# Token factors without a DRAM round trip, four raw and four split weight buffers, values in column halves, head norms on GpSimd's DMA queue: a two-layer hybrid encoder on one Trainium2 core

## The chip, the cores and the metric

One program on one core of one Trainium2 chip. The metric is the device time of one execution in microseconds (us), lower is better. Five engines work at once, each on its own queue in order: PE (TensorE, matmul), DVE (VectorE), ACT (ScalarE), POOL (GpSimd) and SP (SyncE, which here issues DMAs).

## What is computed

Input x is (1, 512, 1024) in float32, so 512 tokens with 1024 columns. Two layers, then a final RMSNorm:

```
h = rmsnorm(x, norm_w)
aq, ak, av, ag, bq, bk, bv, bg, cu, cg = split(h @ w_in)          # 4608 columns
A: 4 heads, two softmax maps each: p = softmax(q k^T / 8 + bias); o = (p0 - lam * p1) @ av; rmsnorm per head; * silu(ag)
B: 4 heads of retention, forward and backward scan with decay, summed; rmsnorm per head; * silu(bg)
C: 4 groups, centred means over 2/4/8/16 tokens minus the token, a 128x128 map, a scale; * silu(cg)
x = x + concat(A, B, C) @ w_out                                    # 1536 rows
```

## The kernel before

**Precision by splitting.** Products run in the array's 4-byte float32r format. Every operand is split into a rounded high part and the rest, `split` (line 453): ACT casts to the high part, DVE subtracts to get the low one. A product is then three matmuls (`mm3`, line 499). So each weight costs one DMA into a raw buffer, one ACT cast and one DVE subtraction before PE can use it.

**Weights.** They stream in granules of 512 KB, 128 partitions by 1024 columns, in the order in which the units use them (`granules`, line 424). `emit_granule` (line 428) loads one into one of 2 `wraw` buffers and splits it into one of WBUFS = 5 pairs `wh`, `wl` (line 25). `take` (line 443) hands out the next granules and records loads up to five granules ahead.

**Order of the work.** The body is recorded first, unit by unit, by the strings in ORDERS (line 32) with the priorities HIGH (line 40). Then a list scheduler (`schedule`, line 201) plays it through with the weights of `cost` (line 304) and the latencies of `LATENCY`, and fixes each engine's instruction order and each tile's buffer. Tiles of one tag get buffers first come, first served in recorded order. So a changed cost, buffer count or operand changes the order of everything after it. All instructions are emitted at line 1051, which is why the profile shows L1051 for nearly all rows; the tile names tell them apart.

**First unit.** `first_values` (line 702) starts layer 0 on x transposed times the norm weight, before the tokens' rms factors are known. START (line 27) is its own order: k0 to k7 are the eight 128-row blocks of x^T with their matmuls, x0 to x3 load the four token tiles and compute their factor into `rc` (128 partitions, one column per tile), R spreads the 512 factors along the free axis into `rb` (128 x 512, every partition the same), V stores the values. R (lines 734 to 737) writes `rc` to DRAM, one 4-byte element at a time in token order, and reads that row back to all partitions, both on SP's queue. `scaled_T` (line 752), `rotated` (line 773) and `c_pool` (line 895) multiply by `rb` in layer 0.

**Values.** `values` (line 694) makes av, and bv of layer 1: 128 tokens are the stationary operand, 512 weight columns move, all four granules of the unit are held at once, and `proj_tok` (line 509) and `store_values` (line 743) go through the four token tiles. The other projections (`proj_T`, line 515) keep 128 weight columns stationary and move 512 tokens.

**Head norm.** `headnorm` (line 538) ends each of the 8 A and 8 B heads: copy out of PSUM, four transposes, squares summed by ACT, a power of -1/2 on POOL, and then the 512 factors go to DRAM and come back to all partitions in `rb`, again on SP's queue, for one DVE multiplication `og<-og,hn`:

```python
        nc.gpsimd.tensor_tensor(st[:, 4:8], st[:, 0:4], neghalf, op=ALU.pow)
        row = nc.tile("dram", "row", [S], 4, F32)
        nc.sync.dma_start(row.rearrange("(p j) -> p j", j=4), st[:, 4:8])
        rb = o
        nc.sync.dma_start(rb, row.partition_broadcast(P))
```

**Attention.** In `a_head` (line 865) one DVE instruction adds the bias to the logits and takes the row maximum, a second one negates that maximum, and ACT takes the exponential with it as its bias.

Of the kernel before, what the change touches and what calls it, by code (L numbers as in the profile page):

```python
# [15 lines left out]
P = 128  # L16
# [8 lines left out]
WBUFS = 5  # L25
# [4 lines left out]
# Order in which the units of a layer are recorded. An output unit is named by the pairs of 128-row blocks of w_out that it takes  # L30
# (A: P Q, B: R S, C: T U) and its half of the columns.
# [7 lines left out]
# how far the units of a kind are moved ahead  # L39
# [4 lines left out]
# The kernel body is recorded first, on tiles that have no place yet. A list scheduler then fixes the order in which  # L44
# every engine issues its instructions and the slot each tile takes, and the program is emitted in that order.
# [17 lines left out]
class View:  # L63
    """Part of a recorded tile: partitions p0..p1, free offsets idx, and the steps that lead to it."""
# [32 lines left out]
    def window(self, row, first, pattern):  # L97
        """DRAM only: elements of a row from first on, by an access pattern of its own."""
        return View(self.base, self.p0, self.p1, self.idx, self.steps + (("window", row, first, pattern),))

    def spread(self, n):
        """Every element n times, along a new last axis."""
        return View(self.base, self.p0, self.p1, np.repeat(self.idx[..., None], n, -1), self.steps + (("spread", n),))
# [47 lines left out]
class Recorder:  # L151
# [49 lines left out]
    def schedule(self):  # L201
# [39 lines left out]
        def ready(op):  # L241
            """A PSUM bank serves one engine at a time."""
            t = op.ready
            for b in op.banks:
                for e, end in b.last.items():
                    if e != op.engine:
                        t = max(t, end + latency(e, op.engine))
            return t
# [3 lines left out]
        while len(order) < len(self.ops):  # L252
# [14 lines left out]
            if e == "SP":  # L267
                bus = max(bus, start + 1100) + op.time
                op.end = bus + 908
# [28 lines left out]
WARM = 16  # matmuls on zeros at the start  # L298
QUEUE = 8  # transfers under way in a queue
FINE = 2  # weight granules of the first columns that come in two parts  # L300
# [3 lines left out]
def cost(engine, method, args, kw):  # L304
    """What an instruction weighs for the list scheduler: until its result stands, and on its engine."""
    out = args[0]
    n = out.idx.size if isinstance(out, View) else 0
    psum = any(isinstance(a, View) and a.base.space == "psum" for a in args)
    if engine == "PE":
# [5 lines left out]
        t = max(107, n * 0.417) + 2.5  # L315
        return t, t
    if engine == "SP":
# [3 lines left out]
        return nbytes / 360.0, 475  # L321
    if engine == "DVE":
# [10 lines left out]
        elif method == "memset":  # L333
            t = 9
        else:
            t = 1.041 * max(n, 2) + 75
        return t, t
    if engine == "ACT":
# [3 lines left out]
        t += 93 * ("accum_out" in kw)  # L342
        return t, t
    if method == "tensor_tensor" and kw["op"] == ALU.pow:
        return 300 + 164 * n, 300 + 164 * n
# [5 lines left out]
def record(ins: dict, out: bass.AP):  # L351
# [46 lines left out]
    ident = sb("ident", [P, P])  # L398

# [6 lines left out]

    def g_out(l, e0, half):
        return w_out[l, e0:e0 + 256, HALF[half]].rearrange("(k p) c -> p k c", p=P)

    def unit_granules(l, u):  # L410
        if u in ("bv", "av"):
            return g_tok(l, BV if u == "bv" else AV)
# [15 lines left out]
    def emit_granule(parts=1):  # L428
        src = granules[len(wt)]
        shp = [P, src.shape[1], src.shape[2]]  # L430
        raw = sb("wraw", shp, 2)
# [11 lines left out]
    def take(n):  # L443
        i = wstate[0]
        wstate[0] += n
        while len(wt) < min(i + WBUFS, len(granules)):
# [12 lines left out]
    def square(t, half, junk, part=None):  # L459
        """Mean square of token tile t: the share of one half of its columns, or of a quarter in the second half."""  # L460
# [14 lines left out]
    def scaled(t, wb, dst, half):  # L475
        """One half of the columns of the rmsnorm of token tile t."""
# [3 lines left out]
    def transpose4(src, step=None):  # L480
        """Four 128-column blocks of src, each transposed, in one bank."""
# [22 lines left out]
    def mm_stacked(ps, qk, m, cols):  # L504
        """Full product of slot m's query columns with its keys: both query parts lie stacked on partitions."""
# [3 lines left out]
    def proj_tok(ps, gs, hh, hl, t):  # L509
        for k in range(KD):  # L510
            wh, wl = gs[k // 2]
            mm3(ps, hh[:, k, t * P:(t + 1) * P], hl[:, k, t * P:(t + 1) * P],
                wh[:, k % 2, :], wl[:, k % 2, :], k == 0, k == KD - 1)
# [8 lines left out]
    def stack_halves(dst, slots, src, scale, dup):  # L522
        """Split the 64 rows of each half of src. Without dup the low part goes to the other partition half of
        the same slot; with dup both parts take a slot each, present on both partition halves."""
# [13 lines left out]
    def headnorm(ov, scale, g):  # L538
        """ov * scale * rsqrt(mean over partitions of ov^2 + eps) * g"""
# [11 lines left out]
        nc.sync.dma_start(row.rearrange("(p j) -> p j", j=4), st[:, 4:8])  # L551
        rb = o
        nc.sync.dma_start(rb, row.partition_broadcast(P))
# [3 lines left out]
    def out_half(ms, half, after=None, before_end=None):  # L557
        """before_end: the last token tile comes in two quarters of the columns, and this follows the first."""
# [25 lines left out]
    def decay_tables():  # L584
        # retention decay rows: log_gamma on 8 partitions (layer, head), columns (forward, backward)
# [33 lines left out]
        # decay of a key to the border of its chunk that faces the other chunk, by token: columns (tile, layer, head)  # L619
# [7 lines left out]
    def column_tables():  # L627
        # per-channel columns: subln (2 rows), pool_scale (8 rows), with the gate's factor 1/2
# [7 lines left out]
    def bias_tables():  # L636
        # relative-position bias by distance
# [8 lines left out]
        for i in range(2):  # L646
            ps = lgp()
            nc.tensor.matmul(ps[0:4, :], rbs, ohr[0:64, HALF[i]], start=True, stop=True)
            nc.vector.tensor_copy(gsb[0:4, HALF[i]], ps[0:4, :])
        nc.sync.dma_start(gdram, gsb[0:4, :])  # L650

        # lambda of each layer
# [13 lines left out]
    def toeplitz(src, row):  # L666
        """t[p, 895 - j] = value at distance j - 384 - p"""
# [4 lines left out]
    def chunk_decay(row):  # L672
        """t[p, j, 255 - c] = decay at distance c - 128 j - p"""
# [4 lines left out]
    def toep_tile(t, i):  # L678
        """[p, c] = value at distance c - 128 i - p"""
        return t[:, i * P:i * P + S][:, ::-1]  # L680

# [1 line left out]
    class Layer:  # L683
# [10 lines left out]
        def values(self):  # L694
            self.vh, self.vl = sb("vh", [P, NT, 512], 1, F32R), sb("vl", [P, NT, 512], 1, F32R)
            gs = take(4)
            for t in range(NT):
                ps = pj()
                proj_tok(ps, gs, self.hh, self.hl, t)
                self.store_values(t, ps)  # L700

        def first_values(self):
            """Layer 0 runs on x^T w; its products take the token's rms afterwards."""
            self.vh, self.vl = sb("vh", [P, NT, 512], 1, F32R), sb("vl", [P, NT, 512], 1, F32R)
            self.rb, self.rc = sb("rb", [P, S]), edge[:, 28:32]
            # the clock of the PE array rises once it has been kept busy for a while
# [6 lines left out]
            for u in START.split():  # L713
# [20 lines left out]
                elif u[0] == "R":  # L734
                    row = nc.tile("dram", "row", [S], 4, F32)
                    nc.sync.dma_start(row.rearrange("(t p) -> p t", t=NT), self.rc)
                    nc.sync.dma_start(self.rb, row.partition_broadcast(P))
# [5 lines left out]
        def store_values(self, t, ps):  # L743
            hi, lo = self.vh[:, t, :], self.vl[:, t, :]
# [7 lines left out]
        def scaled_T(self, ps, scale=1.0):  # L752
            """A product in its final size."""
# [11 lines left out]
        def gate(self, key):  # L765
            """2 silu of the next 128 gate columns."""
# [6 lines left out]
        def rotated(self):  # L773
            """Next 128 columns (two heads), rotated."""
# [18 lines left out]
        def b_qk(self, pr):  # L793
            """Queries and keys of two heads; the state that each of the two chunks hands to the other one."""
# [64 lines left out]
        def a_qk(self, h):  # L859
            t = sb("qk", [P, 6, S], 2, F32R)  # L860
            stack_halves(t, 0, *self.scaled_T(proj_T(self.hh, self.hl), 0.125), False)
# [3 lines left out]
        def a_head(self, h):  # L865
# [3 lines left out]
            for half in range(2):  # L869
                ah, al = ttile([P, NT, 256], F32R), ttile([P, NT, 256], F32R)  # L870
                for i2 in range(2):
# [3 lines left out]
                    for mp in range(2):  # L875
# [3 lines left out]
                        nc.vector.tensor_tensor_reduce(s, lg, toep_tile(bt, i), scale=1.0, scalar=-3e38,  # L879
                                                       op0=ALU.add, op1=ALU.max, accum_out=st[:, mp:mp + 1])  # L880
# [233 lines left out]
```

## Time and profile before

| | before |
|---|---|
| timed runs, us | 682.1, 682.11, 685.32 (median 682.11) |
| span of the profiled execution, us | 679.9 |
| PE busy | 659.5 us, 97% |
| PE weight loads busy (beside PE) | 541.1 us, 80% |
| DVE busy | 500.7 us, 74% |
| ACT busy | 353.9 us, 52% |
| POOL busy | 30.3 us, 4% |
| mean granted PE clock | 0.994 of full speed |
| DMA | 71.86 MB, 106 GB/s over the span |

The span runs from the first to the last instruction. No separate time is given for the profiled execution; the median of the timed runs is 2.2 us above its span, and that is what lies around it. An engine's busy time counts an instruction from its start to its end; matmuls overlap their neighbours in the pipeline, so the rate of PE is read from starts of successive matmuls, not from the duration of one.

### The profile page before, as it was taken

How to read it: one execution, taken by the hardware profiler on the slowest of the kernel's cores; microseconds unless marked ns; L12 is line 12 of the kernel's file. 1: busy time of each engine (PE TensorE's matmuls, PEld its weight loads, DVE VectorE, ACT ScalarE, POOL GpSimd, SP SyncE). 2: the span in 40 equal slices, each digit the busy share in tenths (PEclk: the TensorE clock that was granted, in tenths of full speed). 3: DMA queues.
4: the chain of work that ended last, by engine and by line, in shares of the span. 5: the costliest groups of instructions: out<-in, count | busy, mean ns of one | idle time of the engine just before them, and what ended most of it. 6: DMA issues, size and time to landing. Idle time of an engine off the chain costs nothing.

```text
span 679.9 us, 8912 instructions
## 1 busy us (share of the span) xinstructions
PE 659.5 (97%) x3171; PEld 541.1 (80%) x3171; DVE 500.7 (74%) x954; ACT 353.9 (52%) x701; POOL 30.3 (4%) x51
## 2 busy tenths in 40 slices
PE   9969999999999999999999999899999999999996
PEld 7757887878788888887888888688888887888785
DVE  5468987787787998976574779767568957887733
ACT  7525673434376866553443756344447765655321
POOL 0000000000000000001010000000000000000011
PEclk9979999999999999999999999999999999999999
DMA  9447444323326223243322423532342143224302
GB/s 325 147 127 186 139 115 117 110 94 78 90 50 181 77 91 105 69 115 91 115 63 78 139 64 88 131 118 71 95 122 65 50 150 97 71 92 90 99 31 94
DMA packets 85141, 71.86 MB, mean 106 GB/s; under 512 B 6004, under 2 KB 67604, under 8 KB 85096
## 3 DMA queue, kind: packets, MB, share of 16 engines
q1 hardware_dynamic: 85096, 71.29, 36.3%
q8 instruction: 25, 0.41, 0.2%
q14 instruction: 20, 0.16, 0.1%
HBM read 69.09 MB, written 2.18 MB: 105 GB/s over the span
## 4 chain that ended last, share of the span: by engine, by line
PE 78%; DMA 10%; DVE 6%; issue 2%; ACT 2%; SPq 1%; POOL 0%; POOLq 0%; DVEq 0%; ACTq 0%
PE pj L1051 64%; PE lg L1051 6%; PE ov L1051 4%; PE tp L1051 4%; DMA hn<-row 3%; DMA wide<-dd 2%; DVE qk L1051 1%; DMA row<-edge 1%; DVE soft L1051 1%; DMA wraw<-in_w_in 1%; DVE wl L1051 1%; DMA cols<-in_scales 1%; DMA T<-in_xT_w 1%; DMA x<-in_x 1%; ACT soft L1051 1%
## 5 line engine op out<-in xcount | busy, mean ns | idle before, releaser
L1051 PE MATMUL pj<-hh,wh 128*128 128x512 f32 x448 | 178.5, 400 | 7.9 <-ACT wh L1051 6.5
L1051 PE MATMUL pj<-hl,wh 128*128 128x512 f32 x448 | 177.5, 397 | 0.0
L1051 PE MATMUL pj<-hh,wl 128*128 128x512 f32 x448 | 176.9, 396 | 0.0
L1051 ACT CAST wh<-wraw 128x1024 fp32r<-128x1024 f32 (+1 forms) x97 | 100.8, 1039 | 106.9 <-PE pj L1051 75.8
L1051 DVE TENSOR_TENSOR wl<-wraw,wh 128x1024 fp32r<-128x1024 f32 (+1 forms) x97 | 117.3, 1210 | 29.7 <-ACT wh L1051 29.1
L1051 PEld LDWEIGHTS pj<-hh,wh 128*128 128x128 f32 x448 | 84.7, 189 | 27.1 <-ACT wh L1051 7.0
L1051 PEld LDWEIGHTS pj<-hh,wl 128*128 128x128 f32 x448 | 84.6, 189 | 18.6
L1051 PEld LDWEIGHTS pj<-hl,wh 128*128 128x128 f32 x448 | 84.7, 189 | 17.7
L1051 PE MATMUL pj<-wh,mAC 128*128 128x512 f32 (+1 forms) x264 | 87.5, 391 | 0.0
L1051 ACT ACTIVATE soft<-soft,sm 128x512 f32<-128x512 f32 x96 | 67.8, 718 | 33.9 <-DVE sm L1051 33.5
L1051 DVE TENSOR_TENSOR x<-x,pj 128x512 f32<-128x512 f32 (+1 forms) x65 | 43.6, 675 | 23.2 <-PE pj L1051 22.8
L1051 PEld LDWEIGHTS pj<-wh,mAC 128*128 128x128 f32 x264 | 49.0, 188 | 10.3
L1051 PE MATMUL lg<-qk 128*128 128x512 f32 (+1 forms) x192 | 51.4, 361 | 1.5 <-DVE soft L1051 1.5
L1051 PE MATMUL pj<-wl,mAC 128*128 128x512 f32 (+1 forms) x132 | 51.4, 389 | 0.0
L1051 POOL TENSOR_TENSOR st<-st,neghalf 128x4 f32<-128x4 f32 (+1 forms) x28 | 25.1, 896 | 477.3 <-DVE st L1051 379.2
L1051 DVE CUSTOM_DVE_ANT_0 soft<-lg,wide 128x512 f32<-128x512 f32 x64 | 43.3, 687 | 1.9 <-PE lg L1051 0.3
L1051 PE MATMUL pj<-wh,mB 128*128 128x512 f32 (+1 forms) x136 | 44.5, 383 | 0.0
L1051 PE MATMUL pj<-wh,hl 128*128 128x512 f32 x104 | 41.4, 398 | 0.0
L1051 PE MATMUL pj<-wh,hh 128*128 128x512 f32 x104 | 41.3, 398 | 0.0
L1051 PE MATMUL pj<-wl,hh 128*128 128x512 f32 x104 | 41.2, 396 | 0.0
L1051 PEld LDWEIGHTS lg<-qk 128*128 128x128 f32 x192 | 32.5, 188 | 9.6 <-DVE soft L1051 2.5
L1051 PE MATMUL ov<-T,vh 128*128 128x256 f32 x192 | 39.1, 284 | 0.4 <-DVE og L1051 0.3
(151 smaller groups left out, 949.7 us busy)
## 6 DMA issues: line engine op xcount, KB each, us to landing
wraw<-in_w_in SPq DMA_DIRECT2D x71, 512.0 KB, 4.6
wraw<-in_w_out SPq DMA_DIRECT2D x24, 512.0 KB, 4.1
hn<-row SPq DMA_DIRECT2D x16, 256.0 KB, 3.9
wide<-gd SPq DMA_DIRECT2D x8, 448.0 KB, 4.0
T<-in_xT_w SPq DMA_DIRECT2D x8, 258.0 KB, 4.1
x<-in_x SPq DMA_DIRECT2D x8, 256.0 KB, 5.0
wide<-dd SPq DMA_DIRECT2D x8, 256.0 KB, 4.8
out<-T SPq DMA_DIRECT2D x8, 256.0 KB, 2.1
```

The source lines that it names most:

```text
L1051: op.inst = getattr(getattr(tc.nc, name), method)(*[real(a) for a in op.args], **{k: real(v) for k, v in op.kw.items()})
```

## The change

The factors `rc` are spread into `rb` by a product on PE: four diagonal matrices are made from the identity, split, and multiplied by a matrix of ones. `ones` lies in the one `u` buffer, its float32 original in a `T` buffer. The raw buffers grow from 2 to 4, the split pairs shrink from 5 to 4, and `take` records loads up to six granules ahead. `values` loads and computes its 512 columns in two halves of 256, each from two granules of 512 rows. Head norm's two DMAs move from SP's queue to POOL's. In attention the queries and the bias change sign, so that a row minimum takes the place of the maximum and its negation. The scheduler's costs change as well. (Comments are removed too; that part is left out.)

```diff
-WBUFS = 5
+WBUFS, RBUFS = 4, 4
...
-                op.end = bus + 908
+                op.end = bus + 1100
...
+    crossed = len(args) > 1 and isinstance(args[1], View) and isinstance(out, View) and args[1].p0 != out.p0
...
-        t = max(107, n * 0.417) + 2.5
+        t = max(107, n * 0.4445 + 4)
         return t, t
+    if engine == "POOL" and method == "dma_start":
+        return (1900 if out.base.space == "dram" else 3700), 600
...
-        return nbytes / 360.0, 475
+        return nbytes / 300.0, 475
...
+        t += 117 * crossed
...
-        t += 93 * ("accum_out" in kw)
+        t += 93 * ("accum_out" in kw) + 112 * crossed
...
-        return 300 + 164 * n, 300 + 164 * n
+        return 390 + 160 * n, 390 + 160 * n
...
+    ones = sb("u", [P, UW], 1, F32R)[:, 0:P]
+    onesf = sb("T", [P, 1024], 4)[:, 0:P]
+    nc.vector.memset(onesf, 1.0)
+    nc.vector.tensor_copy(ones, onesf)
...
+    def g_half(l, c):
+        return [w_in[l, g * 512:(g + 1) * 512, c + b * 256:c + b * 256 + 256].rearrange("(k p) c -> p k c", p=P) for b in range(2) for g in range(2)]
...
-            return g_tok(l, BV if u == "bv" else AV)
+            return (g_tok if (l, u) == (0, ORDERS[0][0]) else g_half)(l, BV if u == "bv" else AV)
...
-        raw = sb("wraw", shp, 2)
+        raw = sb("wraw", shp, RBUFS)
...
-        while len(wt) < min(i + WBUFS, len(granules)):
+        while len(wt) < min(i + WBUFS + 2, len(granules)):
...
     def proj_tok(ps, gs, hh, hl, t):
         for k in range(KD):
-            wh, wl = gs[k // 2]
+            wh, wl = gs[k // 4]
             mm3(ps, hh[:, k, t * P:(t + 1) * P], hl[:, k, t * P:(t + 1) * P],
-                wh[:, k % 2, :], wl[:, k % 2, :], k == 0, k == KD - 1)
+                wh[:, k % 4, :], wl[:, k % 4, :], k == 0, k == KD - 1)
...
-        nc.sync.dma_start(row.rearrange("(p j) -> p j", j=4), st[:, 4:8])
+        nc.gpsimd.dma_start(row.rearrange("(p j) -> p j", j=4), st[:, 4:8])
         rb = o
-        nc.sync.dma_start(rb, row.partition_broadcast(P))
+        nc.gpsimd.dma_start(rb, row.partition_broadcast(P))
...
-            nc.vector.tensor_copy(gsb[0:4, HALF[i]], ps[0:4, :])
+            nc.vector.tensor_scalar(gsb[0:4, HALF[i]], ps[0:4, :], -1.0, None, op0=ALU.mult)
...
-            gs = take(4)
-            for t in range(NT):
-                ps = pj()
-                proj_tok(ps, gs, self.hh, self.hl, t)
-                self.store_values(t, ps)
+            for b in range(2):
+                gs = take(2)
+                c = slice(256 * b, 256 * b + 256)
+                for t in range(NT):
+                    ps = pj()[:, c]
+                    proj_tok(ps, gs, self.hh, self.hl, t)
+                    self.store_values(t, ps, c)
...
-                    row = nc.tile("dram", "row", [S], 4, F32)
-                    nc.sync.dma_start(row.rearrange("(t p) -> p t", t=NT), self.rc)
-                    nc.sync.dma_start(self.rb, row.partition_broadcast(P))
+                    dg, dh, dl = soft(), sb("soft", [P, S], 4, F32R), sb("soft", [P, S], 4, F32R)
+                    for t in range(NT):
+                        nc.vector.tensor_scalar(dg[:, t * P:(t + 1) * P], ident, self.rc[:, t:t + 1], None, op0=ALU.mult)
+                    split(dh, dl, dg)
+                    ps = tpp()
+                    nc.tensor.matmul(ps, ones, dh, start=True, stop=False)
+                    nc.tensor.matmul(ps, ones, dl, start=False, stop=True)
+                    nc.scalar.copy(self.rb, ps)
...
-            stack_halves(t, 0, *self.scaled_T(proj_T(self.hh, self.hl), 0.125), False)
+            stack_halves(t, 0, *self.scaled_T(proj_T(self.hh, self.hl), -0.125), False)
...
-                        nc.vector.tensor_tensor_reduce(s, lg, toep_tile(bt, i), scale=1.0, scalar=-3e38,
-                                                       op0=ALU.add, op1=ALU.max, accum_out=st[:, mp:mp + 1])
-                        nc.vector.tensor_scalar(st[:, 2 + mp:3 + mp], st[:, mp:mp + 1], -1.0, None, op0=ALU.mult)
-                        nc.scalar.activation(s, s, AF.Exp, bias=st[:, 2 + mp:3 + mp], accum_out=st[:, 4 + mp:5 + mp])
+                        nc.vector.tensor_tensor_reduce(s, lg, toep_tile(bt, i), scale=1.0, scalar=3e38,
+                                                       op0=ALU.add, op1=ALU.min, accum_out=st[:, mp:mp + 1])
+                        nc.scalar.activation(s, s, AF.Exp, bias=st[:, mp:mp + 1], scale=-1.0, accum_out=st[:, 4 + mp:5 + mp])
...
-                pw = sb("wraw", [P, 8, P], 2)[:, 0:4, :]
+                pw = sb("wraw", [P, 8, P], RBUFS)[:, 0:4, :]
```

## Rows read from the trace of the kernel before

**Rows 1.** The page, first part: busy time, share of the span, instructions.

```profile
PE 659.5 (97%) x3171; PEld 541.1 (80%) x3171; DVE 500.7 (74%) x954; ACT 353.9 (52%) x701; POOL 30.3 (4%) x51
```

**Rows 2.** What PE waited for, whole span: total us, times, longest.

```profile
PE pj L1051 <- ACT wh L1051: 6.5, 1, 6.5
PE lg L1051 <- ACT T L1051: 1.6, 1, 1.6
PE lg L1051 <- DVE soft L1051: 1.5, 2, 1.2
PE pj L1051 <- DVE gate L1051: 1.3, 1, 1.3
```

**Rows 3.** Timeline, 23 to 41 us: start, us, engine, operation, idle before.

```profile
23.95 0.38 SPq L1051 DMA_DIRECT2D row<-edge  x1
...
32.24 0.34 SPq L1051 DMA_DIRECT2D rb<-row  x1
...
32.69 9.25 SPq L1051 DMA_DIRECT2D wraw<-in_w_in  x3
...
37.70 0.69 DVE L1051 TENSOR_TENSOR cos<-cos,rb 128x512 f32<-128x512 f32 x1 [7.48 <-DMA rb<-row]
...
39.05 1.21 DVE L1051 TENSOR_TENSOR wl<-wraw,wh 128x1024 fp32r<-128x1024 f32 x1
...
39.23 1.04 ACT L1051 CAST wh<-wraw 128x1024 fp32r<-128x1024 f32 x1 [9.84 <-DMA wraw<-in_w_in]
...
40.33 0.80 PE L1051 MATMUL pj<-hh,wh 128*128 128x512 f32 x1 [6.54 <-ACT wh L1051]
```

**Rows 4.** Windows of 2 us: PE, PEld, DVE, ACT, POOL busy, granted clock, DMA.

```profile
40.00:42.00 2.00, 1.67 (x4) 1.38 (x5) 2.00 (x5) 0.28 (x1) 0.00 (x0) 0.50 0.23 65
42.00:44.00 2.00, 2.00 (x7) 1.55 (x7) 1.79 (x10) 0.66 (x2) 0.00 (x0) 0.64 0.97 272
```

**Rows 5.** Chain that ended last: start, us, what, instructions.

```profile
292.54 2.85 PE ov L1051 x24
...
352.06 37.49 PE pj L1051 x161
...
633.44 31.60 PE pj L1051 x137
```

**Rows 6.** One head norm, timeline 298 to 308 us.

```profile
298.51 1.01 POOL L1051 TENSOR_TENSOR st<-st,neghalf 128x4 f32<-128x4 f32 x1 [44.84 <-DVE sm L1051]
...
299.54 0.34 SPq L1051 DMA_DIRECT2D row<-st  x1
...
302.12 0.33 SPq L1051 DMA_DIRECT2D hn<-row  x1
...
306.82 0.69 DVE L1051 TENSOR_TENSOR og<-og,hn 128x512 f32<-128x512 f32 x1 [2.53 <-DMA hn<-row]
```

**Rows 7.** Groups of DVE instructions by form: busy us, mean ns, idle before.

```profile
L1051 DVE CAST qk<-qk 64x1024 fp32r<-64x1024 f32 x24 | 16.5, 689 | 0.7
...
L1051 DVE TENSOR_TENSOR og<-og,hn 128x512 f32<-128x512 f32 x16 | 11.1, 691 | 17.6 <-DMA hn<-row 17.4
...
L1051 DVE TENSOR_SCALAR sm<-sm 128x1 f32<-128x1 f32 x64 | 8.7, 147 | 0.0
```

**Rows 8.** What SP's queue waited for: total us, times, longest.

```profile
SPq L1051 <- DVE wl L1051: 302.6, 77, 17.0
...
SPq L1051 <- DMA row<-st: 14.0, 10, 2.8
```

**Rows 9.** Layer change, timeline: PE's first values matmul, DVE's last writes of hl.

```profile
343.43 0.39 PE L1051 MATMUL pj<-wh,hh 128*128 128x512 f32 x1
...
343.62 1.28 DVE L1051 TENSOR_TENSOR hl<-tp,hh 128x512 fp32r<-128x512 f32 x2
...
348.28 1.28 DVE L1051 TENSOR_TENSOR hl<-tp,hh 128x512 fp32r<-128x512 f32 x2
...
352.04 1.36 DVE L1051 TENSOR_TENSOR hl<-tp,hh 128x512 fp32r<-128x512 f32 x2 [0.56 <-ACT hh L1051]
```

More of the change, by code (lines that the diff above doesn't have):

```diff
@@ L741, in first_values, with store_values @@
             wstate[0] = 4
-        def store_values(self, t, ps):
-            hi, lo = self.vh[:, t, :], self.vl[:, t, :]
+        def store_values(self, t, ps, c=slice(0, 512)):
+            hi, lo = self.vh[:, t, c], self.vl[:, t, c]
             if self.rc is None:
```

## The prediction, made before the change was run

> **What bounds the kernel now.** I read the page first: PE is busy 97% of the span, DVE 74%, POOL 4% [rows 1]. So a change that gives DVE or POOL less to do gains only where PE stands still for them. Next, what PE waited for [rows 2]: one wait of 6.5 us stands out, and no other single one is above 1.6 us. The timeline of that moment tells where it comes from [rows 3]. At 23.95 SP issues R's write of the 512 factors, element by element. Its queue then stands until 32.24, when it can issue the read back, and the next weight load follows only at 32.69. The row arrives at 37.70: 13.75 us for a 2 KB vector. Two things that PE needs are stuck behind it and end together: the load on SP's queue (issued 32.69, cast 39.23 + 1.04 = 40.27), and on DVE the subtraction of the weights loaded before, which is queued behind `cos<-cos,rb` (39.05 + 1.21 = 40.26). PE goes on at 40.33. It comes back at half clock: the granted clock is 0.50 in the first window and 0.64 over the second [rows 4], so it is low until about 42 + 2 x 0.36/0.5 = 43.4, and the 3.1 us from 40.33 on do the work of 1.55.
>
> The rest is PE's own rate. In the chain that ended last, 161 matmuls of 512 columns take 37.49 us, 233 ns each, and 137 in the output projection 231 ns; 24 of 256 columns take 2.85 us, 119 ns each [rows 5]. The program has 2432 of 512 columns and 480 of 256; at 232 and 119 ns that is 621 us of the span, and transposes, the start and the tail take most of the rest. No edit here lowers these counts.
>
> **The change part by part.** The sum is made on the profiled execution, span 679.9 us, with 2.2 us around it to the median of 682.11.
>
> *R by a product.* Removed: two DMAs on SP and the hold-up of both queues: -6.5 us of wait and -1.55 of low clock, -8.05. Added: four scalings of a 128x128 diagonal block on DVE. Bounds from the smallest and a large DVE form, 0.147 and 0.689 us [rows 7], nearer to the small one: 0.25 each, 1.0. Then a split of half a granule's size, about half of 1.04 and of 1.21, 1.1; two matmuls of 0.233 on PE; one copy by ACT, about 0.6; with some 1.5 us of hand-overs, about 4.7 us from 23.95, so `rb` stands near 28.7 instead of 37.7. Only the two matmuls, +0.47 us, are certain to cost. They wait on DVE with the first gate's matmuls queued behind them: 0 to 1 us of stall if they are placed too early, taken as 0, since they can stand behind that gate in the order. What is late next? The load held until 32.69 took 6.5 us to its cast. Issued at 24.4 it would be split by 24.4 + 6.5 + 1.04 + 1.21 = 33.2, before the 33.8 at which PE stops now, so nothing follows closely. The ones, memset and copy, are two small DVE instructions while PE waits for its first data: 0 to 0.3, taken as 0.
>
> *Values in halves.* Three units (av twice, bv of layer 1), 288 matmuls, become 576 of 256 columns. By rows 5 a pair costs 2 x 118.8 - 232.9 = 4.7 ns more: 288 x 4.7 = +1.3 us. Twice as many weight loads come with it; the 24 rows of 256 columns already have one load each, so that price is in it. ACT and DVE get 24 short evictions for 12 long ones, hidden under PE. At the layer change there is a new wait. Now a token tile gives 5.6 us of PE work (24 x 233 ns), and the tiles become ready (last `hl`) at about 344.9, 349.6 and 353.4 after a start at 343.43 [rows 9]: each is in time. In halves a tile gives 2.85 us, so the second ends near 349.1 and PE waits 0.5 us for the third and about 1 us for the fourth, unless second-half matmuls are placed between. 0 to 2, taken +1.0.
>
> *Buffers and loads.* Four raw buffers for two let loads run further ahead: SP's queue waits 302.6 us for `wl` to give a raw buffer back [rows 8]. But PE's only wait for a weight is the one at R [rows 2], so this is worth 0. One split pair less shortens the split lead from 5 to 4 granules, 22 us of PE work; values need two granules at a time, so 0, at most +1 in the last output unit, which takes four at once.
>
> *Head norms on POOL's queue.* 32 DMAs leave SP's queue, and with them its 14.0 us wait for the written row [rows 8]. In one chain the write is issued at 299.54, the read at 302.12, and DVE multiplies at 306.82: 7.3 us [rows 6]. POOL's queue gets two issues and that wait; queued behind are the next head's power and the memsets of `u`, on an engine that is 4% busy. Ten or so of the 16 multiplications wait for the row, 17.4 us of DVE [rows 7]. No row has a DMA from POOL. Bounds: at best those 17.4 us go; at worst each chain doubles, +7.3 us. The same bytes move, so I take 0 and keep both ends. What reaches PE: its three waits on or behind DVE chains sum to 4.4 us [rows 2] against those 17.4, so a quarter. By the Trainium skill (DMA: Bandwidth & Descriptors, Specifications) first bytes take about 1 us from GpSimd and 0.6 from SP; by it the estimate is 0.8 us a chain and the sum 2 us higher.
>
> *Negation.* 64 instructions of 147 ns leave DVE, 8.7 us [rows 7], in the shadow of PE: 0, at best -1.
>
> *New order.* Changed costs reorder everything. PE is idle for 679.9 - 659.5 = 20.4 us in all [rows 1]. Without R's 6.5, and with the start and the tail as about half of the rest, some 6 us of small waits are what it can win, 4.4 of them in those three rows; it can lose as much. I take -1.0, since the loads are planned with more latency, and keep -6 and +6.
>
> Sum: -8.05 + 0.47 + 1.3 + 1.0 - 1.0 = -6.3. Span 673.6, time **675.8 us**.
>
> **The rivals.** A measurement here can tell 0.5%, 3.4 us: faster is under 678.7, slower over 685.5.
>
> *Middle waits go too.* Deeper raw buffers and a free SP queue let the order close the 6 us of small waits (-6 in place of -1) and fill the layer change (-1): 669.8. For it: SP's 14.0 us and DVE's 17.4 us. Against it: waits come from DVE's order, not from loads.
>
> *R's wait moves.* `rb` is early, but the first gates and pools find another late thing (DVE must still do the decay tables there, or the new loads compete with x), or the new order gives back what R gains. If 6 of the 8 us come back: 681.8. For it: DVE is busy most of 40 to 44 [rows 4]. Against it: DVE stands 7.48 us idle just before [rows 3].
>
> *The chain lands later on POOL's queue.* A DMA issued by POOL might be held while DVE runs, by 0.689 us (a copy) to 1.21 us (a subtraction) each, besides a longer issue. At the upper bound, +7.3 us on each of ten uncovered chains, DVE waits 73 us more, a quarter of it on PE is +18: 694. It decides once it puts 9.7 us on PE, which is 4 us a chain; below that the gain at R wins. For it: DVE is busy 74%. Against: POOL is nearly idle. The Trainium skill (SBUF — State Buffer, SBUF: two separate sides) says a DVE copy in a two-port mode keeps GpSimd from writing descriptors. No run here shows it. By that rule the 24 copies of 0.689 us, 2.4% of the span, would rarely be hit, hence the low chance.
>
> **How the numbers follow.** Forecast 0.60, middle waits too 0.18, R's wait moves 0.13, late chain 0.09. The forecast's own range is 671 to 680 (order and layer change); with the first rival down to 669 and the second up to 682 some 0.15 is left out. Faster: 0.57 of the forecast and the first rival, 0.75. Same: the forecast's 0.03, 0.12 of the second rival and 0.01 of the third, 0.16. Slower: 0.01 of the second and 0.08 of the third, 0.09.
>
> **What would show it.** PE's 6.5 us wait gone and clock 1.0 from 34 to 44; `rb` written by ACT near 29; head norm's chain near 7 us with its DMAs on a second queue; pairs of 256 columns at 237 ns; a short wait for `hl` at the layer change; small waits of 3 to 9 us in all. Wrong would be a PE wait of several us for weights, or for `og`, that is not there now.

## The result, and the profile after

The forecast was 675.8 us, faster. Measured: **699.97 us** (median of four runs, 699.12 to 703.28) against 682.11, ratio **1.0265 [1.0222, 1.0309]**: slower by 2.65%, outside the range.

The page's first line, and the busy line of the kernel after (answers to rows 1):

```profile
span 701.5 us, 9479 instructions
PE 672.7 (96%) x3461; PEld 559.1 (80%) x3461; DVE 499.9 (71%) x909; ACT 355.9 (51%) x715; POOL 50.4 (7%) x83
```

What PE waited for in the kernel after, whole span, as in rows 2 (total us, times, longest):

```profile
PE tp L1071 <- ACT hn L1071: 3.7, 2, 2.2
PE lg L1071 <- DVE T L1071: 3.4, 1, 3.4
PE lg L1071 <- DVE soft L1071: 3.0, 3, 1.5
PE pj L1071 <- ACT mAC L1071: 2.2, 1, 2.2
PE pj L1071 <- ACT u L1071: 1.9, 1, 1.9
PE pj L1071 <- DVE x L1071: 1.7, 2, 1.4
PE ov L1071 <- DVE T L1071: 1.5, 2, 1.0
```

The one long wait of 6.5 us is gone. In its place stand some ten of 1 to 3.4 us, for DVE or for ACT; the only one for a weight is 1.0 us. All rows of this view together are 14.2 us in 10 waits before and 22.5 us in 19 after: +8.3.

The second part of the loss is the clock. In the profiled execution the mean granted clock fell from 0.994 to 0.982; 0.6% of 679.9 us is 4.1 us not granted, 1.8% of 701.5 is 12.6: at most +8.5 (the clock is also low while PE stands and behind its last matmul). This is the longest of the four executions; the other three were granted 0.988 to 0.992 (spans 697.3 to 698.7 us), so 5.6 to 8.4 us were not granted in them, 1.5 to 4.3 more than before. With the 1.7 us of added matmuls that the prediction has (0.47 + 1.3), the waits and the clock make 18.5 of the 21.6 us by which the profiled span grew. Most of the other 3.1 are gaps too short for the view of waits. Successive matmuls of 512, 256 and 128 columns usually start 231, 118 and 110 ns apart; at full clock and behind the first 12 us, what exceeds that by 25 to 300 ns sums to 9.0 us in 103 gaps before and 11.7 us in 136 after.

**Where the waits come from.** The timeline of the kernel after, one head norm, 302 to 314 us (answers to rows 6):

```profile
302.85 1.03 POOL L1071 TENSOR_TENSOR st<-st,neghalf 128x4 f32<-128x4 f32 x1 [45.18 <-DVE st L1071]
...
304.29 0.61 POOL L1071 DMA_DIRECT2D row<-st  x1 [0.41 <-POOL st L1071]
...
308.53 0.54 POOL L1071 DMA_DIRECT2D hn<-row  x1 [3.63 <-DMA row<-st]
...
312.01 0.69 DVE L1071 TENSOR_TENSOR og<-og,hn 128x512 f32<-128x512 f32 x1 [4.73 <-DMA hn<-row]
...
312.87 0.58 ACT L1071 COPY hn<-ov 128x512 f32<-128x512 f32 x1 [6.31 <-DVE og L1071]
...
313.50 0.75 PE L1071 MATMUL tp<-ident,hn 128*128 128x128 f32 x4 [2.21 <-ACT hn L1071]
```

Read it from the bottom up. PE waits 2.21 us for a copy by ACT; ACT has waited 6.31 us for DVE's `og`; DVE has stood 4.73 us for the row from DRAM. The row came 8.1 us after the power ended (303.88 to 312.01); the order had put the multiplication where it would have come earlier, and what stands behind it in DVE's and ACT's queues comes late too. DVE's group `og<-og,hn`, and what SP's and POOL's queues waited for, in the kernel after (answer to rows 7 and 8):

```profile
L1071 DVE TENSOR_TENSOR og<-og,hn 128x512 f32<-128x512 f32 x16 | 11.0, 690 | 28.2 <-DMA hn<-row 28.1
```

```profile
SPq L1071 <- DVE wl L1071: 382.2, 71, 15.0
...
POOL hn L1071 <- DMA row<-st: 23.2, 9, 3.6
```

DVE's wait for the row is 28.1 us against 17.4, in ten multiplications both times. The 64 negations of rows 7 are gone. SP still waits for `wl` above all, now 382.2 us: four raw buffers fill as two did.

**The clock after short waits.** Windows of 2 us of the kernel after, columns as in rows 4, around DVE's wait of 3.61 us for a row, which left PE waiting 3.39 us for `T` until 445.89:

```profile
444.00:446.00 2.00, 0.11 (x1) 0.11 (x1) 1.25 (x3) 0.59 (x2) 0.00 (x0) 0.70 0.04 14
446.00:448.00 2.00, 2.00 (x7) 1.81 (x8) 1.94 (x4) 1.20 (x3) 0.00 (x0) 0.50 0.00 0
448.00:450.00 2.00, 2.00 (x6) 1.52 (x6) 2.00 (x3) 0.39 (x1) 0.00 (x0) 0.50 0.28 102
450.00:452.00 2.00, 2.00 (x7) 1.57 (x6) 0.07 (x1) 0.00 (x0) 0.00 (x0) 0.59 0.84 233
452.00:454.00 2.00, 2.00 (x11) 1.60 (x10) 0.00 (x0) 0.00 (x0) 0.00 (x0) 1.00 0.44 165
```

From 446 to 452 PE is busy, and nearly half of its clock is not granted: 6 or 7 matmuls in 2 us against 11 at full clock. That is 2 x (0.50 + 0.50 + 0.41) = 2.8 us, nearly as much as the wait.

**R.** The same stretch as rows 3, in the kernel after:

```profile
24.56 0.29 DVE L1071 TENSOR_SCALAR soft<-ident,edge 128x128 f32<-128x128 f32 x1
...
28.12 0.29 DVE L1071 TENSOR_SCALAR soft<-ident,edge 128x128 f32<-128x128 f32 x1
...
28.71 0.61 ACT L1071 CAST soft<-soft 128x512 fp32r<-128x512 f32 x1
...
29.37 0.51 PE L1071 MATMUL tp<-soft,u 128*128 128x512 f32 x1 [0.41 <-ACT soft L1071]
...
31.68 0.59 ACT L1071 COPY rb<-tp 128x512 f32<-128x512 f32 x1
32.78 0.67 DVE L1071 TENSOR_TENSOR cos<-cos,rb 128x512 f32<-128x512 f32 x1
```

`rb` is there at 32.27, 5.4 us before its time in rows 3. The tail of the chain that ended last keeps its rate (rows 5: 37.49):

```profile
652.41 37.42 PE pj L1071 x161
```

### The profile page after: what moved, and what is told of

The parts are those of the page before. It is cut to its first block, busy times and chain, and to the rows that moved or that the text cites. A ratio compares the mean times of both kernels' runs of the same rounds, so it can differ in the third digit from the quotient of the medians.

```text
span 701.5 us, 9479 instructions
## 1 busy us (share of the span) xinstructions
PE 672.7 (96%) x3461; PEld 559.1 (80%) x3461; DVE 499.9 (71%) x909; ACT 355.9 (51%) x715; POOL 50.4 (7%) x83
## 5 line engine op out<-in xcount | busy, mean ns | idle before, releaser
L1071 PE MATMUL pj<-wl,hh 128*128 128x256 f32 (+1 forms) x200 | 58.6, 293 | 0.0
L1071 PE MATMUL pj<-wh,hh 128*128 128x256 f32 (+1 forms) x200 | 57.8, 289 | 0.0
L1071 PE MATMUL pj<-wh,hl 128*128 128x256 f32 (+1 forms) x200 | 57.3, 287 | 0.0
L1071 DVE TENSOR_TENSOR x<-x,pj 128x512 f32<-128x512 f32 (+1 forms) x65 | 43.5, 674 | 16.9 <-PE pj L1071 16.6
L1071 PEld LDWEIGHTS lg<-qk 128*128 128x128 f32 x192 | 30.6, 192 | 15.9 <-issue 6.7
```

Source lines behind the costliest of these rows:

```text
L1071: op.inst = getattr(getattr(tc.nc, name), method)(*[real(a) for a in op.args], **{k: real(v) for k, v in op.kw.items()})
```

## The experiments

The letters in the expectations: P or S, prices in the order's plan that leave no slack; Q, the chains on GpSimd's queue; H, the halves or the buffers; W, that the halves lose at one place in layer 0. "Price" is always a number in `cost` or in `schedule`: it moves instructions and adds none. Ratios are to the kernel before in runs on the same chip.

**1. After, head norm's DMAs back on SP (order made anew).**

```diff
-        nc.gpsimd.dma_start(row.rearrange("(p j) -> p j", j=4), st[:, 4:8])
+        nc.sync.dma_start(row.rearrange("(p j) -> p j", j=4), st[:, 4:8])
...
-        nc.gpsimd.dma_start(rb, row.partition_broadcast(P))
+        nc.sync.dma_start(rb, row.partition_broadcast(P))
```

> The changed kernel with head norm's two DMAs back on SP's queue, all else as changed; the order is planned anew. Theory Q (the chain of the head norm lands later than the order assumes, because it is on GpSimd's queue with a price of 1.9 + 3.7 us): most of the 18 us of lost time comes back, near 683 us, and PE's waits fall from 23 to about 15 us. Theory S (with PE priced at its true rate the order has no slack left): little comes back, 694 us or more. Theory H (buffers and halves are the loss): about 700 us.

Measured 1.0100 [1.0076, 1.0124], which is 688.9 us on the scale of 682.11: between Q's 683 and S's 694, so neither came in. The move, with its price, has a share of the loss, not all of it.

**2. After, PE's old price.**

```diff
-        t = max(107, n * 0.4445 + 4)
+        t = max(107, n * 0.417) + 2.5
```

> The changed kernel with one line of the scheduler's costs as before: a 512-column matmul is priced at 216 ns instead of 231.6. Not one instruction is added or removed, only the order can change. Theory S: the order then plans results earlier than PE needs them, so the time falls by 8 us or more, below 692. Theory Q: the chains stay short of time, 695 to 700. Theory H: 700, unchanged.

Measured 1.0130 [1.0097, 1.0163], 691.0 us on the same scale, as S said: a price alone has about half of the loss.

**3. Before, PE's new price alone** (the reverse edit of 2; not one instruction differs from the kernel before).

> The kernel before with the changed price of a matmul alone (231.6 ns instead of 216 for 512 columns). Theory S: it becomes slower by 8 to 13 us, near 692, through small PE waits that are not there before. Theories Q and H: nothing of theirs is in it, so 682 within 3 us.

Measured **1.0243** [1.0212, 1.0274]. What PE waited for in it:

```profile
PE pj L1051 <- ACT wh L1051: 4.2, 1, 4.2
PE pj L1051 <- DVE soft L1051: 3.6, 1, 3.6
PE tp L1051 <- ACT hn L1051: 2.8, 4, 1.3
PE tp L1051 <- DVE soft L1051: 1.8, 3, 1.2
```

The truer price makes the order worse, by nearly as much as the whole change did and by more than the 8 to 13 us that S named (2.43% of 682.11 is 16.6). Of the 18.9 us by which the profiled span grew, the view of waits has 9.1 (23.3 against 14.2); another 5.3 are the short gaps described above (14.3 us in 158). The old formula gives 216 ns for 512 columns, the new one 231.6; rows 5 show 231 to 233. The reading, which 6 puts to a test: PE priced 7% too fast made the plan want every operand early, which covered the transfers that are priced too short; at the true rate the plan has everything arrive just in time, by prices at which it doesn't.

**4. Before, R by the product alone** (the edit in `first_values` and the ones, as in the change).

> The kernel before with the tokens' factors spread by the product on PE, nothing else. The step of the prediction on R says -8.05 + 0.47, so 674.5. Were it the case that any new order loses here what R gains, it would be 682 or more.

Measured **0.9873** [0.9855, 0.9891]: -1.27% of 686.2, -8.7 us. The prediction's two terms for R gave -7.6.

**5. After, GpSimd's DMAs priced dearer.**

```diff
-        return (1900 if out.base.space == "dram" else 3700), 600
+        return (2800 if out.base.space == "dram" else 4700), 600
```

> The changed kernel with GpSimd's DMAs priced at 2.8 and 4.7 us instead of 1.9 and 3.7, about what its trace shows from issue to use; no instruction added or removed. Theory P (the order is planned with prices under which results come just in time, and the head norm's DMAs are priced too low): the waits on head norms go, ratio to before about 1.00, near 0.02 lower than the changed kernel. Theory Q (the queue itself is slow): the chain takes as long, so at most 0.005 of the 0.0265 comes back.

Measured **1.0015** [0.9998, 1.0033], from 1.0265. Two numbers, no instruction. DVE's wait for the row falls with it:

```profile
L1071 DVE TENSOR_TENSOR og<-og,hn 128x512 f32<-128x512 f32 x16 | 11.0, 687 | 6.3 <-DMA hn<-row 6.3
```

**6. Before, PE's new price, and a transfer's landing priced 1 us later.** It tests the reading of 3: if the slack was what PE's old price gave, another price must give it back.

```diff
-                op.end = bus + 908
+                op.end = bus + 1908
```

> The kernel before with the new price of a matmul, which alone made it slower by 0.024, and with the time that a transfer on SP's queue needs to land priced 1 us higher (908 to 1908 ns); again only the order changes. Theory P: PE's price hurt because transfers were priced short beside it, so with both raised the loss goes, ratio 1.00 or below. If instead any order other than the tuned one loses: 1.02 or more.

Measured 1.0067 [1.0042, 1.0091], from 1.0243: most of it comes back, but not all; P had 1.00 or below. The strings in ORDERS and the priorities HIGH stayed the same in every run here; whether others would suit the true price better was not tested.

**7. After, in exactly its order, the 32 DMAs emitted on SP at the same places.** Only the queue differs (1 also made a new order).

```diff
+            if name == "gpsimd" and method == "dma_start":
+                name = "sync"
```

> The changed kernel in exactly its own order, only that head norm's 32 DMAs are issued at the same places by SP instead of GpSimd. Theory Q: the chains become shorter by some 1 us each and the time falls by 8 us or more, to a ratio of 1.015 or less. Theory P: the waits are in the order, not in the queue; what changes is 0.9 us in each of some ten chains, a quarter of it on PE, so 1.02 to 1.03.

Measured 1.0106 [1.0071, 1.0142], against 1.0265: in this order the queue is worth 1.6%. That is Q's range, and P, which wanted 1.02 to 1.03, missed it; by 5, though, most of the same loss goes with the DMAs left on POOL, if the plan allows more time for them. From the end of the power to `og`, the mean of the ten chains for which DVE waited is 7.15 us here and 7.7 after; before it is 6.8. So the queue costs about 0.6 us a chain in the same order, 0.9 against before. On POOL the issue takes 0.61 and 0.54 us (0.34 and 0.33 in rows 6) and begins 0.3 to 0.4 us after the power (0.02 in rows 6); the read's time from issue to landing is no longer (median 3.6 us, 3.9 before, 4.6 in this run). The PE waits are 17.4 us against 22.5 and the clock 0.992 against 0.982 in the profiled executions: small lateness, passed on and enlarged.

**8. The quiet base: before, R by the product (4), and landings priced 1908.**

> The kernel before with the factors spread by the product on PE and with landing priced 1 us higher for the order (908 to 1908 ns). Theory P: besides R's 9 us some of the small waits go, ratio 0.975 to 0.985 against 0.987 with R alone. If prices do not matter here, 0.987; if any new order loses, 1.00.

Measured **0.9746** [0.9720, 0.9772], PE waits 3.9 us in all, clock 0.997. With nearly no waits left, it shows what each part costs by itself.

**9. Quiet base + values in halves** (the edits in `granules`, `proj_tok`, `values` and `store_values`, as in the change).

> Values in column halves alone, on the kernel of e8 (before, R by the product, landing priced 1 us higher; ratio 0.9746, few small waits left). Theory H (halves cost more than the prediction's 2.3 us of extra issue and layer change): ratio 0.983 or more, 6 us and up, with the waits around the values and the layer change. The prediction's own price: 0.978.

Measured 0.9886 [0.9865, 0.9907], span 677.5 against 666.5: +11, which is what H said (0.983 or more). One place has most of it, in attention of layer 0. Counted from the starts of successive matmuls, as what exceeds the usual spacing, PE has lost as much as in the quiet base at 126 us (3.1 and 3.2), 2.4 us more at 140 (6.9 and 4.5), and 8.7 us more at 190 (15.5 and 6.8). So the place, from 172 to 190, has 6.2. The 2.4 us before it go with a wait of PE for `mAC` that ends at 130.15 (1.38 us, 0.40 in the quiet base) and a granted clock of 0.55 and 0.60 in the windows from 132 and 134. The timeline of the place, kernel with halves:

```profile
171.55 1.05 ACT L1065 CAST wh<-wraw 128x1024 fp32r<-128x1024 f32 x1 [4.52 <-PE pj L1065]
...
172.91 1.23 DVE L1065 TENSOR_TENSOR wl<-wraw,wh 128x1024 fp32r<-128x1024 f32 x1 [2.26 <-ACT wh L1065]
...
173.12 0.28 PE L1065 MATMUL pj<-wh,hl 128*128 128x256 f32 x1
...
178.21 1.19 PE L1065 MATMUL lg<-qk 128*128 128x512 f32 x2 [4.81 <-DVE soft L1065]
```

and the quiet base at the same point of its work, some 2.4 us earlier on its clock:

```profile
174.54 0.40 PE L1060 MATMUL pj<-wh,hh 128*128 128x512 f32 x1
174.83 0.70 PE L1060 MATMUL lg<-qk 128*128 128x512 f32 x2
...
176.65 0.40 PE L1060 MATMUL pj<-wh,hl 128*128 128x512 f32 x1
```

Both kernels make the operands of the first attention heads on ACT and DVE here, which takes them some 9 us. In the quiet base PE fills this time with the values' matmuls of 512 columns; its first wait in the view is one of 0.64 us, at 180.60. With halves the first half's matmuls are used up at 173.12. The second half's start at 184.12, behind the logits: the granule cast at 171.55, which waited 4.52 us for PE to give a `wh` buffer back, is split only at 174.14, when the order has already turned to the logits. So PE stands 4.81 us and comes back at a lower clock (mean 0.66 from 175 to 185). That the late buffer is why the plan put the second half so late is argued from these rows; more split pairs were not tried.

**10. Quiet base + four raw and four split buffers, six granules ahead.**

> Four raw and four split buffers and loads recorded six granules ahead, alone, on the kernel of e8 (0.9746). The prediction priced this at 0: 0.9746 within 0.003. Theory H (the shorter split lead and the earlier splits on ACT and DVE cost): 0.98 or more.

Measured 0.9732 [0.9710, 0.9755]: no difference from 8.

**11 and 12. Quiet base + head norms on POOL's queue,** priced 2800 and 4700 (11), or 1900 and 3700 as in the change (12).

> Head norm's DMAs on GpSimd's queue, priced 2.8 and 4.7 us for the order, alone, on the kernel of e8 (0.9746). Theory P (the queue does no harm where its price is right): 0.973 to 0.978. Theory Q (the chains of the queue are late whatever the order): 0.985 or more.

> As e11, with the changed kernel's prices of 1.9 and 3.7 us for GpSimd's DMAs, so that only the order differs from e11. Theory P: 0.985 to 0.995, by waits on head norms, though nothing but two numbers of the planner differs from e11. If prices do not matter: as e11.

Measured 0.9723 [0.9703, 0.9742] and **0.9924** [0.9891, 0.9958]. The same instructions on the same queues: 2% lies in two prices, and the move itself costs nothing where the plan allows for it. DVE's group of head norms, with the dear price and with the change's:

```profile
L1062 DVE TENSOR_TENSOR og<-og,hn 128x512 f32<-128x512 f32 x16 | 11.0, 686 | 10.7 <-DMA hn<-row 10.5
L1062 DVE TENSOR_TENSOR og<-og,hn 128x512 f32<-128x512 f32 x16 | 11.0, 690 | 24.4 <-DMA hn<-row 24.3
```

With the dear price four multiplications wait for their row, with the change's eleven. PE's waits with the dear price:

```profile
PE pj L1062 <- ACT mAC L1062: 1.6, 2, 0.9
PE tp L1062 <- DVE soft L1062: 1.4, 1, 1.4
PE tp L1062 <- ACT hn L1062: 0.4, 1, 0.4
```

and with the change's:

```profile
PE tp L1062 <- ACT hn L1062: 5.6, 2, 3.0
PE pj L1062 <- ACT mAC L1062: 2.6, 1, 2.6
PE tp L1062 <- DVE soft L1062: 2.2, 2, 1.4
PE lg L1062 <- ACT T L1062: 1.0, 1, 1.0
```

Two of the waits of the kernel after come back, those for `hn` and `mAC`, with DVE's long waits for the row.

**13. After with the dear queue (5) and values at full width.**

> The changed kernel with two of its parts taken back: GpSimd's DMAs priced 2.8 and 4.7 us for the order, and values at full width. If these two are all of the loss, what is left is R's gain and some order: ratio 0.975 to 0.985. If something else in the change costs as well (PE's new price, the buffers): 0.99 or more.

Measured 0.9915 [0.9885, 0.9946], span 675.6: something else costs as well. The halves' 1% goes, as in 9, but 9.6 us of span stay to 11 (666.0). PE's waits are only 4.0 us longer (7.4 against 3.4) and the clock is the same (0.998); 4.7 us of the rest are short gaps (12.6 us in 146, against 7.9 in 88).

**14. Quiet base, halves in layer 1 only.**

> e9 (ratio 0.9886 against 0.9746 without halves) with the halves in layer 1 only; av of layer 0 is at full width. Theory W (the loss of the halves is one place in layer 0: ACT's and DVE's next weight split stands in their queues waiting for a split pair that the first half gives back, and the queries behind it come late): 0.975 to 0.979. Theory H (every unit in halves costs): two thirds of the loss stay, 0.984 or more.

Measured 0.9806 [0.9771, 0.9841], span 668.0: 1.5 us above the quiet base; by the ratios it is 0.006, some 4 us, on another chip. That lies between the ranges of W and H. Until the end of layer 0 this kernel is no later than the quiet base (its last power there begins at 337.80 against 338.10), and 9 is 9.6 us later (347.75), so that part of 9's 11 us comes with layer 0's one unit in halves. That a weight split waiting in ACT's and DVE's queues is the reason, as W has it, stays argued.

**15. Run 11 + the change of sign in attention.**

> e11 (before, R by the product, landing priced 1 us higher, head norms on GpSimd's queue at 2.8 and 4.7 us; 0.9723) with the change's sign trick, which takes 64 small instructions off DVE. The prediction priced that at 0: 0.970 to 0.9735.

Measured 0.9742 [0.9711, 0.9773], **665.81 us**, no change from 11; its span, 663.3, is the lowest of all.

```profile
PE 655.3 (99%) x3173; PEld 540.3 (81%) x3173; DVE 497.3 (75%) x897; ACT 355.7 (54%) x703; POOL 49.0 (7%) x83
```

PE waits 2.0 us in all. Runs 8, 10, 11 and 15 each beat both kernels; their intervals overlap, so none is shown to be the best.

**16 and 17. Run 13 with PE's old price (16), or with the landing priced 1908 (17).** They ask which price makes the 9.6 us of 13.

> The kernel after, with GpSimd's DMAs priced 2800 and 4700 ns and values at full width (the kernel that took 0.9915 of before), and now PE's old price, max(107, 0.417 n) + 2.5 ns for n columns, in place of 0.4445 n + 4. No instruction changes, only the order. Theory 'PE's price': the 10 us between that kernel and the quiet one with the dear queue (span 675.6 against 666.0) come from PE priced at its true rate while a load is priced short; ratio 0.970 to 0.978, span 664 to 669. Rival 'landing': they come from the loads' landing price of 1100 in place of 1908 ns, which is still in it; 0.988 or more, span 674 or more. Rival 'rest' (DMA bandwidth, evictions' prices): no change either, 0.99, here and in the next run.

> The same kernel (after, GpSimd's DMAs at 2800 and 4700 ns, values at full width) with PE's new price kept and the loads' landing priced 1908 ns in place of 1100. Theory 'PE's price': the new price takes the slack away, and a dearer landing gives a part of it back, as it did on the kernel before (2.43% slower, 0.67% with the dearer landing); ratio 0.976 to 0.990, span 666 to 676. Rival 'landing': 0.970 to 0.976, span 664 to 668. Rival 'rest': unchanged, 0.99.

Measured **0.9769** [0.9740, 0.9798], span 669.5, and 0.9862 [0.9823, 0.9901], span 675.4. PE's price makes 6.1 of the 9.6 us by the spans, 0.0146 of 0.0192 by the ratios: its theory came in, and in 17 'rest' can't be told from it. The dearer landing, which helped the kernel before so much (6), can't be told from nothing here: 17's interval overlaps 13's. Of the spans 3.5 us are left; by the ratios 16's interval touches 11's. In 16 one place is as large as that, a wait of PE for a weight's cast near R that 11 doesn't have:

```profile
30.23 0.50 PE L1069 MATMUL pj<-hh,wh 128*128 128x512 f32 x1 [2.00 <-ACT wh L1069]
```

The granted clock behind it is 0.71 in the window from 30 to 32 and 0.50 from 32 to 34. Counted as in 9, PE has lost 6.9 us by 60 us in 16 and 2.8 in 11, and 14.1 and 10.6 at the end: the 3.5 us are all lost near R. Which price puts the wait there is not shown.

## Why the prediction was wrong, by its own steps

**The failing step is "New order", taken as -1.0 with bounds of -6 and +6, together with the 0 for the head norms on POOL's queue.** The text read the changed prices as a reshuffle around a mean near nothing, a little better because "the loads are planned with more latency". The loads are, but the reshuffle has a sign: PE's price alone is +2.4% (3), and the queue's two prices +2.0% (12 against 11) or 2.5% (after against 5), either of them more than the bound of 6 us. The two overlap: by 2, PE's price is worth half of the loss in the kernel after.

What the profile could have told beforehand: prices can be held against rows. The new prices allow 1.9 us for the write and 3.7 for the read, 5.6 together. Rows 6 had 2.58 from write to read (299.54 to 302.12) and 4.70 from read to use, 7.3 together on the faster queue; on POOL it is 4.24 and 3.48 in the chain shown, up to 5.3 for the read in others. So the plan is short by 1 to 2 us on each of 16 chains. The rows alone would not have given the size, though: the old prices were shorter still. By the formulas in `cost` and `schedule` SP's write and read came to 4.8 us at least (2 x (1100 + 908) ns, and their bytes at 360 a ns), and the kernel before lost 14.2 us to waits with them. New in the change are the longer chain on POOL's queue and PE's price, whose low value, in 3's reading, covered for the short ones.

**R by a product, -8.05 + 0.47: right.** Alone it measured -8.7 us, and in the kernel after the 6.5 us wait is gone. `rb` came at 32.27 and not near 28.7, since the fourth token tile's factor is ready only at 28.1; it cost PE 0.41 us. The 1.0 us wait for a weight's cast stands just before it (until 28.23).

**Values in halves, +1.3 and +1.0: the first right, the second in the wrong place.** Successive starts of 256-column matmuls are 0.118 us apart in the kernel after. In layer 1, which has the layer change and two units in halves, the whole price is 1.5 us of span (14; 4 us by the ratios). At the layer change PE lost 0.34 us in the kernel after:

```profile
357.20 0.28 PE L1071 MATMUL pj<-wh,hh 128*128 128x256 f32 x1
...
357.82 0.63 PE L1071 MATMUL tp<-ident,T 128*128 128x128 f32 x4 [0.34 <-DVE T L1071]
```

What was missed is layer 0: 9.6 us of span by 9, 6.2 of them at the place in attention, where a half feeds PE for 4 x 2.85 = 11.4 us and the whole unit fed it for 22.4. "Values need two granules at a time, so 0" looked at whether PE's weights are there in time, not at what PE does while attention's operands are made.

**Buffers, 0: right** (10). **Negation, 0, at best -1: right** as far as it can be told (15 against 11: span -2.7 us, ratio 0.0019 higher, intervals overlapping).

**Head norms on POOL's queue, 0 between "all waits go" and "each chain doubles".** The queue adds about 0.9 us to a chain against before, 0.6 in the same order. By the Trainium skill (DMA: Bandwidth & Descriptors, Specifications) the estimate was 0.8 us a chain; the trace agrees in size. It has the time before and in the issue, not between issue and landing (7). The 2 us that the prediction worked out for the sum were not enough for this order: emitted on SP in the same order, the profiled execution is 8.0 us of span shorter (7). The quarter of DVE's waits that the text let reach PE was too small: DVE's wait grew by 6.1 us (22.0 to 28.1) from run 7 to the kernel after, PE's by 5.1. The mean granted clock was 0.991 to 0.994 in the four executions of 7 and 0.982 to 0.992 in those of the kernel after.

**The rivals.** "The chain lands later on POOL's queue" named the right place and sign. Its mechanism was not seen: it needed 4 us a chain, and the time to landing is the same on both queues. That the plan would count on an earlier row than the queue gives was not among the rivals, and it should have been: the diff has the prices in it. "R's wait moves" had the nearest words, "the new order gives back what R gains", but it stopped at 6 of R's 8 us, 681.8; the new order took back all of them and 18 us more. "Middle waits go too" falls; yet runs 8, 11 and 15 show that those waits can be closed, by dearer transfers. The prediction's own sign of being wrong did show: PE waits of 2.2 and 3.4 us behind a late row.

What settles that prices make the loss is 2, 3, 5, 12 and 16, in which only prices differ. Why the true price of PE makes a worse order is the reading given at 3: 6 bears it out in part, 17 doesn't. What stays open besides is which of the smaller prices (bandwidth, evictions) makes the 3.5 us near R that 16 still has over 11.

## What to carry to other kernels

Where a static plan fixes every queue's order, a price in it is part of the program: before forecasting, hold each changed price against the row that it stands for, and ask which other error it was balancing. Correcting one of two errors that cancel can make the plan worse (3). Correcting the other as well gave most of it back (6), but in each pair run here the plan with PE's lower price stayed the faster one (2, 3, 16), so a truer price is to be tried like any other edit. Price a transfer at its slow end: some 1 us more cost nothing in these runs (8, 11, 17), and too cheap puts an in-order engine in front of an empty buffer. A wait of DVE for a transfer is PE's wait as soon as PE's next operands stand behind it.

## What the runs showed of the hardware beyond that

PE's clock fell after waits far shorter than the 6.5 us of rows 2, though not after all. In the kernel after, a wait of 2.19 us that ended at 130.22 and the one of 3.39 us at 445.89 were followed by a granted clock of 0.50, and one of 2.21 us at 313.50 (the head norm above) by 1.00. Windows of the two that are alike in length:

```profile
130.00:132.00 2.00, 1.75 (x4) 1.13 (x5) 1.97 (x4) 1.11 (x2) 0.00 (x0) 0.70 0.00 0
132.00:134.00 2.00, 2.00 (x6) 1.58 (x5) 1.14 (x2) 0.00 (x0) 0.00 (x0) 0.50 0.16 25
...
312.00:314.00 2.00, 0.49 (x4) 0.50 (x5) 1.29 (x2) 1.13 (x2) 0.00 (x0) 1.00 0.00 0
314.00:316.00 2.00, 2.00 (x12) 1.64 (x11) 1.49 (x3) 1.97 (x10) 0.01 (x1) 1.00 0.02 4
```

The length of the wait alone doesn't tell which it will be. The wait of 1.87 us that ended at 471.72 was followed by 0.53 and 0.62 in the windows from 472 and 474. Another low stretch, 0.50 in the windows from 182 to 188 and 0.80 in the next, came after 4 us in which PE was busy for 1.62 us, though no wait in them was longer than 1.35 us. In this execution the small waits were in sum about twice as dear as their length, up to 8.5 us of clock beside 8.3 us of waits. That is the upper end: with the clocks of the other three executions, 0.988 to 0.992, the same sum gives 1.5 to 4.3 us of clock.
